# Two feed-forward blocks and a mixer on one core: a separate ring for the second products' left operands, exchanged accumulators, later transposes, and a last norm split in two

## The chip, the cores and the metric

The kernel runs on one core of a Trainium2 chip. The metric is device time in microseconds (us): 2611.52 us is the median of three runs of the kernel before (2611.07 to 2611.73). The profile is of one more execution, which took 2607.64 us, with 2605.9 us from its first instruction to its last.

## The reference

One trunk layer is computed for 128 context tokens and 1024 latent tokens of width 1024. Cut to what matters here:

```python
def _swiglu(h, w1, w2):                       # D_FF = 2816
    a, b = jnp.split(h @ w1, 2, axis=-1)
    return (jax.nn.silu(a) * b) @ w2

def _layer(x, mod, lw, rope, kv_ctx):
    sh1, sc1, g1, sh2, sc2, g2, sh3, sc3, g3 = [mod[:, i][:, None, :] for i in range(N_MOD)]
    f1 = _swiglu(_modulate(x, sh1, sc1), lw['ffn1_w1'], lw['ffn1_w2'])
    x = _layer_norm(ALPHA * x + 0.5 * g1 * f1, lw['ln_g'][0], lw['ln_b'][0])
    mix, k, v = _mixer(_modulate(x, sh2, sc2), lw, rope, kv_ctx)
    x = _layer_norm(ALPHA * x + g2 * mix, lw['ln_g'][1], lw['ln_b'][1])
    f2 = _swiglu(_modulate(x, sh3, sc3), lw['ffn2_w1'], lw['ffn2_w2'])
    x = _layer_norm(ALPHA * x + 0.5 * g3 * f2, lw['ln_g'][2], lw['ln_b'][2])
```

`_mixer` projects x, makes queries and keys with an RMS norm and a rotary turn, runs attention and a pooling branch, and projects the gated sum. Everything is float32.

## The kernel before

Every float32 operand is split into a high part (copied by ScalarE, L109) and a low part (subtracted by VectorE, L110), and each product is three matmuls (`mm3`, L132, L133, L134): high by high, high by low, low by high. `split` makes both parts, `transpose` (L137) is a matmul with the identity.

Each feed-forward block has an *up* stage and a *down* stage. The up stage makes silu(a)*b for the latent tokens with a Strassen scheme of seven products for a two by two blocking, and stores the parts and their sums (`keep_h`, `h_sums`: tiles `tmp`, `raw`, `pc`) to the tensor `h` in DRAM through POOL's DMA queue. The context tokens' feed-forward (`ctx_ffn`) runs in between as side work, advanced by `tick`. The down stage is h @ w2 with the same scheme: seven products M1, M5, M6, M7, M4, M3, M2 in this order, each of six groups; a group is two 128-row blocks of w2 for four row tiles, 24 matmuls of 128x512, and the last group one block, 12. For a group, `left` loads a part of h into a `raw` tile and splits it into two `so` tiles; `right` loads a piece of w2 into a `raw` tile, for M5 also a second one whose difference goes into a `tc` tile, and splits it into two `op` tiles. All these loads go through SP's queue in program order and share the five `raw` tiles of the pool `feed`. The last groups of a product (`tail`) are kept back and run tile by tile, and `done` takes the accumulators away. Each finished row tile is normed by `norm` in three steps, as side work, and the last product's norms in the last stage run at once.

The first down stage ends with `x_from_dram` as side work (`order`): it loads the normed x again into `raw` tiles, transposes it for the mixer and modulates it. The mixer's `queries` transposes the rotated queries `qr` just after they are made, and `ctx_attention` transposes the probabilities `pr` in the same way. The third norm stage ends the program.

What order the instructions have on an engine is decided when the program is built: the engines' queues are in order, pools hand out tiles in a ring, and a tile placed over the space of an older pool's tiles waits for the last use of those, a store's landing among them.

Of the kernel before, what the change touches and what calls it, by code (L numbers as in the profile page):

```python
# [25 lines left out]
F32 = mybir.dt.float32  # L26
F32R = mybir.dt.float32r
# [5 lines left out]
P = 128  # L33
D = 1024
# [20 lines left out]
class Layer:  # L55
# [203 lines left out]

    def modulate(self, slot, src, i, kc, g):  # L260
        m = self.raw_tile()[:, :GT]
        if g == 0:
            self.modulated(m[:, :P], src[:, :P], i, CTX, kc)
            self.modulated(m[:, P:], src[:, P:], i, LAT, kc)
        else:
            self.modulated(m, src, i, LAT, kc)
        self.split(slot[:, 0, :], slot[:, 1, :], m)

    def x_from_dram(self, src, i, g, out):
# [166 lines left out]
    def ctx_ffn(self, i, x, w1c, w1t, w2):  # L436
# [5 lines left out]
        for c in range(6):  # L442
# [5 lines left out]
            nc.scalar.activation(h[:, :n], banks[0][:, :n], AF.Silu)  # L448
            nc.vector.tensor_tensor(h[:, :n], h[:, :n], banks[1][:, :n], ALU.mult)
            if acc is None:  # L450
                acc = [self.bank(), self.bank()]
# [201 lines left out]
    def down(self, i, w2, h_d, norms, order, half, last):  # L653
# [3 lines left out]
        groups = [(f, min(2, 11 - f)) for f in range(0, 11, 2)]  # L657
        ops = lambda: self.pools["so"].tile([P, 1024], F32R, tag="so", name=self.name("so"), bufs=14 if last else 6)
        where = {"M1": 0, "M2": 2, "M4": 3, "M6": 4, "M5": 5, "M3": 6, "M7": 7}
        chain = [None] * len(groups)  # L660

        def left(name, g):
            c = groups[g][1]
            r = self.raw(h_d[g][:, where[name], :c, :], c * 512)
            hi, lo = ops()[:, : c * 512], ops()[:, : c * 512]
            self.split(hi, lo, r)
            return hi, lo
# [49 lines left out]
        yt = lambda: self.t([P, 2, 512], "y", bufs=8, pool=self.pools["y"])  # L717
        copy = lambda out, b: nc.scalar.activation(out, b, AF.Copy)
        X = [self.bank() for _ in range(4)]
        Y = [self.bank() for _ in range(4)]  # L720
        y1, y2 = ([yt() for _ in range(4)] for _ in range(2))
# [14 lines left out]

        def done1(j):
            add(y1[j][:, 0, :], Z[j], y1[j][:, 0, :])
            g = norm(half[0] + j, y1[j], fine=last and j == 3)
            if last:  # L740
                for _ in g:
                    pass
            else:
                self.add_side(g)

        if order:
            self.add_side(order())
        product("M2", Z, True, done1, tail=6 if last else 2, ticks=3)
        self.flush()
# [7 lines left out]
    def norms(self, i, res_of, dst):  # L757
# [7 lines left out]

        def norm(t, y, fine=False):
            y = self.flat(y)
            gate = gc if t == 0 else gl
            res = self.t([P, D], "res", bufs=2)
            with self.tc.issue_after(self.last_load):  # L770
                nc.sync.dma_start(res, res_of(t))
            rs = self.t([P, 1], "rs")
            mu = self.t([P, 1], "mu")
            nc.vector.tensor_tensor(y, y, gate, ALU.mult)
            yield
            nc.vector.scalar_tensor_tensor(y, res, ALPHA, y, ALU.mult, ALU.add, accum_out=mu)
            nc.vector.tensor_scalar(mu, mu, -1.0 / D, None, ALU.mult)  # L777
            nc.scalar.activation(res, y, AF.Square, bias=mu, accum_out=rs)
            nc.gpsimd.tensor_scalar(rs, rs, 1.0 / D, EPS, ALU.mult, ALU.add)
            nc.gpsimd.tensor_tensor(rs, rs, self.mhalf[:, 0:1], ALU.pow)  # L780
            yield
            for cs in [slice(0, 512), slice(512, D)] if fine else [slice(0, D)]:
                nc.vector.scalar_tensor_tensor(y[:, cs], y[:, cs], mu, lg[:, cs], ALU.add, ALU.mult)
                nc.vector.scalar_tensor_tensor(y[:, cs], y[:, cs], rs, lb[:, cs], ALU.mult, ALU.add)
                (nc.sync if last_stage(i) else nc.gpsimd).dma_start(dst(t)[:, cs], y[:, cs])
            yield

        return norm

    def ffn(self, i, head, res_of, dst, order, half, beside=None):  # L790
# [19 lines left out]
        with ExitStack() as st:  # L810
            self.open_pools(st, "down" + s, ("op", "tc", "so", "y", "rest") if i == 0 else ("op", "tc", "y", "rest", "so"))
            self.ph = self.pools["rest"]
            self.down(i // 2, a["w2_" + s], h_d, lambda: self.norms(i, res_of, dst), order, half, last_stage(i))
# [154 lines left out]
    def queries(self, g, acc, qg, pq):  # L968
        nc = self.nc
        for j in range(3):  # L970
# [13 lines left out]
            self.rope(qn, qr, self.rope_table(3 * g + j, 0, qg, pq), 8, pq)  # L984
            yield
            for h in range(2):
                b = self.bank()
# [134 lines left out]
    def ctx_attention(self, pool):  # L1122
        nc = self.nc
        for kvh in range(2):
# [15 lines left out]
            nc.vector.reciprocal(sm, sm)  # L1140
            nc.vector.tensor_tensor(pr, pr, sm.unsqueeze(2).broadcast_to([P, 4, P]), ALU.mult)
            yield
            b2 = self.bank()
# [148 lines left out]
    def run(self):  # L1292
# [3 lines left out]
        with ExitStack() as right:  # L1296

            def beside():
# [3 lines left out]
                0, self.head_input, lambda t: a["x"][self.rows(t)], lambda t: self.x1_d[t // 3][:, t % 3],  # L1302
                lambda: self.x_from_dram(self.x1_d, 1, 0, x), (5, 1), beside,
            )
# [39 lines left out]
def last_stage(i):  # L1344
    return i == 2
# [107 lines left out]
```

## Time and profile before

| | value |
|---|---|
| median of three runs | 2611.52 us (2611.07 to 2611.73) |
| the profiled execution | 2607.64 us |
| its span | 2605.9 us |
| mean granted TensorE clock | 0.976 |
| TensorE busy | 2481.7 us (95%) |
| VectorE busy | 1833.2 us (70%) |
| ScalarE busy | 1215.5 us (47%) |
| GpSimd busy | 458.4 us (18%) |

The span counts from the first to the last instruction; the profiled execution took 1.74 us more. TensorE idles for 124.2 us in all, and a granted clock of 0.976 means that for a part of the span its matmuls run at half speed. Every stage has its own pattern: the up stage of the first block ends at about 579 us, its down stage at 820, the mixer's input projection at 1265, its attention at 1560, its output at about 1855, the second up stage at 2358, and the second down stage's last matmul is at 2583. After that only the last norms run.

### The profile page before, as it was taken

How to read it: one execution, taken by the hardware profiler on the slowest of the kernel's cores; microseconds unless marked ns; L12 is line 12 of the kernel's file. 1: busy time of each engine (PE TensorE's matmuls, PEld its weight loads, DVE VectorE, ACT ScalarE, POOL GpSimd, SP SyncE). 2: the span in 40 equal slices, each digit the busy share in tenths (PEclk: the TensorE clock that was granted, in tenths of full speed). 3: DMA queues.
4: the chain of work that ended last, by engine and by line, in shares of the span. 5: the costliest groups of instructions: out<-in, count | busy, mean ns of one | idle time of the engine just before them, and what ended most of it. 6: DMA issues, size and time to landing. Idle time of an engine off the chain costs nothing.

```text
span 2605.9 us, 34155 instructions
## 1 busy us (share of the span) xinstructions
PE 2481.7 (95%) x12226; PEld 2133.9 (82%) x12226; DVE 1833.2 (70%) x2802; ACT 1215.5 (47%) x2086; POOL 458.4 (18%) x671
## 2 busy tenths in 40 slices
PE   7999999999998999999899999998999999999996
PEld 3788788877787989989899999997788788887775
DVE  4877688875686745577888876765777667666686
ACT  4644444434345343434578773433644444434442
POOL 0000001010011311132467640110000001110001
PEclk8999999999998999999999999999999999999998
DMA  7355567767666854445300024554455446558674
GB/s 283 113 181 179 165 229 237 245 229 235 208 225 236 234 174 165 162 150 174 109 1 2 1 78 164 202 209 156 139 196 180 159 165 238 198 195 266 231 234 141
DMA packets 164338, 461.64 MB, mean 177 GB/s; under 512 B 18804, under 2 KB 34932, under 8 KB 164168
## 3 DMA queue, kind: packets, MB, share of 16 engines
q1 hardware_dynamic: 143368, 383.63, 44.3%
q0 software_dynamic: 20800, 75.84, 8.0%
q8 instruction: 96, 1.57, 0.2%
q14 instruction: 74, 0.61, 0.1%
HBM read 388.32 MB, written 71.07 MB: 176 GB/s over the span
## 4 chain that ended last, share of the span: by engine, by line
PE 78%; DVE 8%; DMA 7%; issue 3%; ACT 2%; POOL 1%; SPq 1%; DVEq 0%; POOLq 0%; ACTq 0%
PE w L133 22%; PE w L132 22%; PE w L134 22%; PE w L861 7%; DMA raw<-w 4%; PE w L137 3%; DVE op L110 2%; DMA raw<-h 1%; DVE so L110 1%; DVE mx L1168 1%; DVE junk L192 1%; PE w L226 1%; DVE x L110 1%; DMA raw<-x 0%; SPq L113 0%
## 5 line engine op out<-in xcount | busy, mean ns | idle before, releaser
L109 ACT ACTIVATE op<-raw 128x1024 fp32r<-128x1024 f32 (+1 forms) x505 | 484.4, 970 | 606.2 <-PE w L133 265.2
L110 DVE TENSOR_TENSOR op<-raw,op 128x1024 fp32r<-128x1024 f32 (+1 forms) x505 | 558.6, 1113 | 267.3 <-ACT op L109 236.9
L132 PE MATMUL w<-b,op 128*128 128x512 f32 x880 | 342.4, 391 | 4.4 <-DVE tmp L546 2.4
L133 PE MATMUL w<-b,op 128*128 128x512 f32 x880 | 343.2, 390 | 0.3 <-DVE b L110 0.3
L134 PE MATMUL w<-b,op 128*128 128x512 f32 x880 | 341.4, 390 | 1.9 <-DVE op L110 1.9
L132 PE MATMUL w<-x,op 128*128 128x384 f32 x768 | 264.2, 345 | 4.3 <-ACT pin L1018 2.3
L134 PE MATMUL w<-x,op 128*128 128x384 f32 x768 | 261.0, 342 | 3.2 <-DVE mu L777 2.6
L133 PE MATMUL w<-x,op 128*128 128x384 f32 x768 | 261.9, 341 | 0.0
L134 PE MATMUL w<-op,so 128*128 128x512 f32 x616 | 244.2, 401 | 8.9 <-DVE so L110 8.9
L132 PE MATMUL w<-op,so 128*128 128x512 f32 x616 | 241.8, 401 | 8.8 <-ACT op L109 4.2
L133 PE MATMUL w<-op,so 128*128 128x512 f32 x616 | 245.5, 399 | 1.7 <-DVE op L110 1.7
L487 POOL DMA_DIRECT2D h<-tmp x80 | 43.5, 544 | 905.7 <-DVE tmp L551 440.5
L132 PEld LDWEIGHTS w<-b,op 128*128 128x128 f32 x880 | 165.7, 188 | 40.5 <-DVE tmp L546 3.3
L134 PEld LDWEIGHTS w<-b,op 128*128 128x128 f32 x880 | 165.5, 188 | 36.9 <-DVE op L110 2.3
L133 PEld LDWEIGHTS w<-b,op 128*128 128x128 f32 x880 | 165.6, 188 | 34.4 <-DVE b L110 0.6
L1181 POOL TENSOR_TENSOR pr<-pr,sm 128x384 f32<-128x384 f32 x192 | 157.5, 850 | 93.3 <-DVE sm L1179 75.8
L132 PE MATMUL w<-ax,op 128*128 128x512 f32 x352 | 136.1, 402 | 19.0 <-ACT ax L109 16.1
L132 PEld LDWEIGHTS w<-x,op 128*128 128x128 f32 x768 | 146.8, 191 | 6.2 <-ACT op L109 3.4
L192 DVE SCALAR_TENSOR_TENSOR junk<-raw,sil 128x1024 bf16<-128x1024 f32 x112 | 140.2, 1259 | 14.3 <-DMA raw<-w_mod 13.7
L134 PEld LDWEIGHTS w<-x,op 128*128 128x128 f32 x768 | 146.5, 191 | 3.9 <-DVE op L110 3.9
L134 PEld LDWEIGHTS w<-op,so 128*128 128x128 f32 x616 | 118.7, 193 | 37.5 <-DVE so L110 11.3
L132 PEld LDWEIGHTS w<-op,so 128*128 128x128 f32 x616 | 118.6, 193 | 36.8 <-ACT op L109 5.1
(269 smaller groups left out, 5098.2 us busy)
## 6 DMA issues: line engine op xcount, KB each, us to landing
raw<-w SPq DMA_DIRECT2D x240, 256.0 KB, 4.0
raw<-w SPq DMA_DIRECT2D x116, 512.0 KB, 4.2
raw<-h SPq DMA_DIRECT2D x92, 512.0 KB, 4.5
raw<-w1c SPq DMA_DIRECT2D x80, 512.0 KB, 4.5
raw<-w_mod SPq DMA_DIRECT2D x56, 512.0 KB, 4.3
raw<-w_gate SPq DMA_DIRECT2D x48, 512.0 KB, 4.2
h<-tmp POOLq DMA_DIRECT2D x80, 256.0 KB, 4.0
h<-pc POOLq DMA_DIRECT2D x52, 256.0 KB, 4.5
```

The lines of the kernel that those rows point to most:

```text
L109: self.nc.scalar.activation(hi, src, AF.Copy)
L110: self.nc.vector.tensor_tensor(lo, src, hi.bitcast(F32), ALU.subtract)
L132: mm(out, lhsT=lh, rhs=rh, start=start, stop=False)
L133: mm(out, lhsT=lh, rhs=rl, start=False, stop=False)
L134: mm(out, lhsT=ll, rhs=rh, start=False, stop=stop)
L137: self.nc.tensor.transpose(out, src, self.ident)
L192: nc.vector.scalar_tensor_tensor(junk, w, 1.0, self.sil[cond], ALU.mult, ALU.mult, accum_out=self.mod[:, cond, b : b + 1],)
L226: nc.tensor.matmul(acc[:2, :256], lhsT=self.sil_t[:, :, lo + k], rhs=w[:, k, :], start=lo + k == 0, stop=lo + k == KC - 1,)
L487: self.nc.gpsimd.dma_start(h_d[f // 2][:, 2 * kh + n, f % 2, :], h)
L861: self.nc.tensor.matmul(acc[h][j], lhsT=lhs[:, part, js], rhs=w[wi][:, h * 512 : (h + 1) * 512], start=f, stop=l)
L1168: nc.vector.tensor_reduce(mx[:, c : c + 1], b[:, :GT], AX.X, ALU.max)
L1181: nc.gpsimd.tensor_tensor(pr[:, c, :], pr[:, c, :], sm[:, 3:4].broadcast_to([P, GT]), ALU.mult)
```

## The change

The left operands of the down stages' products are loaded into a ring `sr` of their own (three tiles in the first stage, four in the last) in place of `raw` tiles. The `op` ring of the down stages has 6 tiles in the first and 12 in the last (8 before in both), and the `so` ring of the last stage 12 (14 before), so the pools lie in other places. The accumulators X and Y are allocated in the other order. The first stage's side work at its end becomes `x_early`, which loads x through POOL's queue into a ring `xr` of two, waits for eight ticks, and transposes in eight steps during M2. `queries`, `ctx_attention` and `ctx_ffn` get one more `yield` each, by which their transposes come one tick later. In the last stage tile 3's norm is split: `last` multiplies what is already summed by the gate and adds the residual, for each half of the row, before M2, and `finish` multiplies M2's accumulator by the gate, adds it and does what is left of the norm, in halves; its y goes out by the queues of SP and ScalarE. The other norms store through POOL's queue.

```diff
+    def x_early(self, src, i, out, wait):
+        t = lambda tag, n: self.pools["xr"].tile([P, n], F32, tag=tag, name=self.name(tag), bufs=2)
+        def load(q):
+            r = t("xr", 768)
+            self.nc.gpsimd.dma_start(r.rearrange("p (a b) -> p a b", a=3), src[0][:, :, q * 256 : (q + 1) * 256])
+            return r
+        r = [load(0), load(1)]
+        for _ in range(wait):
+            yield
+        for q in range(4):
+            for k in range(2):
+                b = self.bank()
+                for j in range(3):
+                    self.transpose(b[:, j * P : (j + 1) * P], r[q][:, j * 256 + k * P : j * 256 + (k + 1) * P])
+                s = self.xslot()
+                self.modulate(s, b[:, :GT], i, 2 * q + k, 0, t("xm", GT))
+                out.append(s)
+                if k and q < 2:
+                    r.append(load(q + 2))
+                yield
...
@@ ctx_ffn
             nc.vector.tensor_tensor(h[:, :n], h[:, :n], banks[1][:, :n], ALU.mult)
+            yield
...
@@ down
-        ops = lambda: self.pools["so"].tile([P, 1024], F32R, tag="so", name=self.name("so"), bufs=14 if last else 6)
+        ops = lambda: self.pools["so"].tile([P, 1024], F32R, tag="so", name=self.name("so"), bufs=12 if last else 6)
...
-            r = self.raw(h_d[g][:, where[name], :c, :], c * 512)
+            r = self.pools["sr"].tile([P, 1024], F32, tag="sr", name=self.name("sr"), bufs=4 if last else 3)[:, : c * 512]
+            self.load(r.rearrange("p (a b) -> p a b", a=c), h_d[g][:, where[name], :c, :])
...
+        Y = [self.bank() for _ in range(4)]
         X = [self.bank() for _ in range(4)]
-        Y = [self.bank() for _ in range(4)]
...
         def done1(j):
+            if last and j == 3:
+                finish(Z[j])
+                return
             add(y1[j][:, 0, :], Z[j], y1[j][:, 0, :])
-            g = norm(half[0] + j, y1[j], fine=last and j == 3)
+            g = norm(half[0] + j, y1[j])
...
+        def last(t, y):
+            tt, stt = nc.vector.tensor_tensor, nc.vector.scalar_tensor_tensor
+            res = residual(t)
...
+            for (v, cs), out in zip(halves, (None, m2)):
+                tt(v, v, gl[:, cs], ALU.mult)
+                stt(v, res[:, cs], ALPHA, v, ALU.mult, ALU.add, accum_out=out)
+            def finish(b):
+                z = res[:, c0]
+                tt(z, b, gl[:, c0], ALU.mult)
+                stt(y0, z, 1.0, y0, ALU.mult, ALU.add, accum_out=mu)
+                nc.vector.tensor_scalar(mu, mu, m2, -1.0 / D, ALU.add, ALU.mult)
+                nc.scalar.activation(res, self.flat(y), AF.Square, bias=mu, accum_out=rs)
+                for v, cs in halves:
+                    stt(v, v, mu, lg[:, cs], ALU.add, ALU.mult)
+                nc.gpsimd.tensor_scalar(rs, rs, 1.0 / D, EPS, ALU.mult, ALU.add)
+                nc.gpsimd.tensor_tensor(rs, rs, self.mhalf[:, 0:1], ALU.pow)
+                for (v, cs), q in zip(halves, (nc.sync, nc.scalar)):
+                    stt(v, v, rs, lb[:, cs], ALU.mult, ALU.add)
+                    q.dma_start(dst(t)[:, cs], v)
+            return finish
...
@@ ffn
-            self.open_pools(st, "down" + s, ("op", "tc", "so", "y", "rest") if i == 0 else ("op", "tc", "y", "rest", "so"))
+            self.open_pools(st, "down" + s, ("op", "tc", "so", "y", "sr", "xr", "rest") if i == 0 else ("op", "tc", "sr", "y", "rest", "so"))
+            self.op_bufs = 6 if i == 0 else 12
...
@@ queries
             yield
+            if j == 0:
+                yield
...
@@ ctx_attention
             nc.vector.tensor_tensor(pr, pr, sm.unsqueeze(2).broadcast_to([P, 4, P]), ALU.mult)
+            yield
             yield
...
@@ run
-                lambda: self.x_from_dram(self.x1_d, 1, 0, x), (5, 1), beside,
+                lambda: self.x_early(self.x1_d, 1, x, 8), (5, 1), beside,
```

Three places show how instructions move. The first is VectorE's queue where the first down stage begins. `pc_851` and `pc_852` are the last sums of h that the up stage makes, `op_880` and `op_886` are low parts of right operands, `so_889` that of a left operand (group 3 of M1), and `tc_909` is the first difference of M5's. Before:

```order
568 L110 TENSOR_TENSOR op_880_4674<-raw_878_4670,op_879_4673 128x1024
569 L110 TENSOR_TENSOR op_886_4711<-raw_884_4707,op_885_4710 128x1024
570 L502 TENSOR_TENSOR pc_851_4580<-tmp_848_4529,raw_850_4575 128x512
571 L502 TENSOR_TENSOR pc_852_4583<-tmp_845_4509,raw_850_4575 128x512
572 L110 TENSOR_TENSOR op_892_4748<-raw_890_4744,op_891_4747 128x1024
573 L110 TENSOR_TENSOR so_889_4741<-raw_887_4738,so_888_4740 128x1024
```

And now, where `so_871`, `so_877` and `so_883` are the left operands' low parts of M1's groups 0, 1 and 2 (before, they stood ahead of row 568):

```order
566 L110 TENSOR_TENSOR op_886_4717<-raw_884_4713,op_885_4716 128x1024
567 L527 TENSOR_TENSOR pc_851_4580<-tmp_848_4529,raw_850_4575 128x512
568 L527 TENSOR_TENSOR pc_852_4583<-tmp_845_4509,raw_850_4575 128x512
569 L707 TENSOR_TENSOR tc_909_4855<-raw_910_4856,raw_908_4852 128x1024
570 L110 TENSOR_TENSOR so_871_4636<-sr_869_4633,so_870_4635 128x1024
571 L110 TENSOR_TENSOR so_877_4673<-sr_875_4670,so_876_4672 128x1024
572 L110 TENSOR_TENSOR so_883_4710<-sr_881_4707,so_882_4709 128x1024
573 L707 TENSOR_TENSOR tc_917_4897<-raw_918_4898,raw_916_4894 128x1024
574 L110 TENSOR_TENSOR so_889_4747<-sr_887_4744,so_888_4746 128x1024
575 L110 TENSOR_TENSOR op_892_4754<-raw_890_4750,op_891_4753 128x1024
```

The low parts of M1's left operands moved behind the stage's last sums of h and behind a difference for M5 (rows 569 and 573), which needs two loads of w2. The load of `raw_910` waits on SP for `pc_852` and for the landing of the store of `raw_850`, whose place it takes.

The second place is ScalarE's queue where the last down stage begins; `tmp_4018` is the up stage's last silu, the `so` tiles are left, the `op` tiles right operands' high parts. Before:

```order
1744 L550 ACTIVATE tmp_4018_21139<-w_4002_20984 128x512
1745 L109 ACTIVATE so_4039_21194<-raw_4038_21192 128x1024
1746 L109 ACTIVATE op_4042_21201<-raw_4041_21198 128x1024
1747 L109 ACTIVATE so_4045_21231<-raw_4044_21229 128x1024
1748 L109 ACTIVATE op_4048_21238<-raw_4047_21235 128x1024
```

And now:

```order
1744 L575 ACTIVATE tmp_4018_21147<-w_3997_20974 128x512
1745 L109 ACTIVATE so_4039_21205<-sr_4038_21203 128x1024
1746 L109 ACTIVATE so_4045_21242<-sr_4044_21240 128x1024
1747 L109 ACTIVATE so_4051_21279<-sr_4050_21277 128x1024
1748 L109 ACTIVATE so_4057_21316<-sr_4056_21314 128x1024
1749 L109 ACTIVATE so_4063_21353<-sr_4062_21351 128x1024
1750 L109 ACTIVATE so_4069_21366<-sr_4068_21364 128x512
1751 L109 ACTIVATE op_4042_21212<-raw_4041_21209 128x1024
```

The first right operand moved behind all six left ones. On VectorE its low part `op_4043` follows in the same way, and its place was that of the tile `pc_4021`, so it waits for the landing of that tile's store.

The third place is TensorE's queue in the first down stage, where M2 begins; `w_1117` to `w_1120` are its four accumulators. Before:

```order
3110 L134 MATMUL w_1120_6030<-op_1125_6040,so_1123_6034 128x512
3111 L137 MATMUL w_1128_6070<-ident_75,raw_1127_6068 128x128 x3
3112 L137 MATMUL w_1131_6080<-ident_75,raw_1127_6068 128x128 x3
3113 L137 MATMUL w_1135_6092<-ident_75,raw_1134_6090 128x128 x3
3114 L137 MATMUL w_1144_6139<-ident_75,raw_1134_6090 128x128 x3
3115 L137 MATMUL w_1148_6151<-ident_75,raw_1147_6149 128x128 x3
3116 L137 MATMUL w_1151_6161<-ident_75,raw_1147_6149 128x128 x3
3117 L132 MATMUL w_1117_6027<-op_1142_6111,so_1139_6104 128x512
```

And now:

```order
3111 L137 MATMUL w_1141_6152<-ident_75,xr_1127_6074 128x128
3112 L132 MATMUL w_1117_6033<-op_1133_6087,so_1130_6080 128x512
3113 L132 MATMUL w_1118_6034<-op_1133_6087,so_1130_6080 128x512
3114 L132 MATMUL w_1119_6035<-op_1133_6087,so_1130_6080 128x512
3115 L132 MATMUL w_1120_6036<-op_1133_6087,so_1130_6080 128x512
3116 L137 MATMUL w_1141_6152<-ident_75,xr_1127_6074 128x128 x2
3117 L137 MATMUL w_1150_6199<-ident_75,xr_1127_6074 128x128 x3
3118 L137 MATMUL w_1154_6211<-ident_75,xr_1128_6076 128x128
3119 L133 MATMUL w_1117_6033<-op_1134_6088,so_1130_6080 128x512
```

Of the eighteen transposes that stood ahead of M2's first group seven are still there, the others moved behind later groups of it (eleven in rows 3187 to 3190, six more in rows 3221 and 3222 with the six that followed later before).

## Rows read from the trace of the kernel before

**Rows 1.** The profile page, its first line.

```profile
span 2605.9 us, 34155 instructions
```

**Rows 2.** Stages: window, length, busy by engine, clock, DMA share, GB/s.

```profile
579.00:820.00 241.00, 223.20 (x948) 181.74 (x948) 152.91 (x161) 101.23 (x132) 18.00 (x20) 0.96 0.67 226
2584.00:2605.90 21.90, 0.00 (x0) 0.00 (x0) 17.04 (x24) 4.97 (x8) 6.64 (x8) 0.60 0.42 144
```

**Rows 3.** What TensorE waited for: line, releaser, total us, times, longest us.

```profile
PE w L137 <- DMA raw<-x: 13.9, 5, 7.2
PE w L134 <- DVE so L110: 8.9, 4, 3.4
PE w L137 <- DVE qr L932: 6.5, 3, 3.1
PE w L137 <- DVE pr L1141: 4.6, 1, 4.6
PE w L132 <- DVE y L725: 2.9, 2, 2.3
PE w L134 <- DVE mu L777: 2.6, 1, 2.6
```

**Rows 4.** TensorE's timeline, first down stage: start, us, instruction, idle before.

```profile
579.49 1.20 PE L132 MATMUL w<-op,so 128*128 128x512 f32 x4 [1.63 <-ACT op L109]
582.47 0.63 PE L133 MATMUL w<-op,so 128*128 128x512 f32 x1
582.89 0.63 PE L134 MATMUL w<-op,so 128*128 128x512 f32 x1
```

**Rows 5.** Short stretches, columns as in rows 2.

```profile
579.40:593.60 14.20, 13.66 (x52) 10.87 (x53) 9.34 (x10) 5.81 (x7) 2.37 (x4) 0.88 0.82 280
584.60:593.60 9.00, 9.00 (x41) 7.47 (x40) 4.14 (x4) 3.88 (x4) 1.11 (x2) 0.99 0.96 332
784.00:799.00 15.00, 7.77 (x31) 6.35 (x29) 7.17 (x10) 11.13 (x22) 0.00 (x0) 0.77 0.66 199
1118.00:1128.20 10.20, 7.11 (x29) 6.73 (x28) 7.66 (x11) 3.73 (x8) 4.62 (x7) 0.67 0.34 109
```

**Rows 6.** DMA issues, 581.5 to 590: transfer, queue, count, KB, median landing us.

```profile
raw<-w SPq DMA_DIRECT2D x4, 256.0 KB, 4.0
h<-raw POOLq DMA_DIRECT2D x1, 512.0 KB, 4.4
h<-pc POOLq DMA_DIRECT2D x2, 256.0 KB, 6.3
```

**Rows 7.** Timeline of POOL's queue and VectorE, first down stage.

```profile
581.98 0.72 POOL L499 DMA_DIRECT2D h<-raw  x1 [1.91 <-DVE raw L498]
588.91 1.22 DVE L110 TENSOR_TENSOR so<-raw,so 128x1024 fp32r<-128x1024 f32 x1
607.02 1.23 DVE L681 TENSOR_TENSOR tc<-raw,raw 128x1024 f32<-128x1024 f32 x1 [3.96 <-DMA raw<-w]
614.71 1.22 DVE L681 TENSOR_TENSOR tc<-raw,raw 128x1024 f32<-128x1024 f32 x1 [4.10 <-DMA raw<-w]
```

**Rows 8.** Timeline of three engines, start of the last down stage.

```profile
2360.65 0.80 PE L133 MATMUL w<-op,so 128*128 128x512 f32 x1 [1.24 <-DVE op L110]
2361.65 1.29 DVE L502 TENSOR_TENSOR pc<-tmp,raw 128x512 f32<-128x512 f32 x2
2362.63 0.57 POOL L503 DMA_DIRECT2D h<-pc  x1 [2.15 <-DVE pc L502]
```

**Rows 9.** Timeline of four engines, end of the program.

```profile
2582.92 0.40 PE L134 MATMUL w<-op,so 128*128 128x512 f32 x1
2598.11 1.15 ACT L778 ACTIVATE res<-y,mu 128x1024 f32<-128x1024 f32 x1 [3.49 <-DVE mu L777]
2600.27 0.94 POOL L780 TENSOR_TENSOR rs<-rs,mhalf 128x1 f32<-128x1 f32 x1
2601.24 1.42 DVE L784 SCALAR_TENSOR_TENSOR y<-y,rs,nc 128x512 f32<-128x512 f32 x2 [0.44 <-POOL rs L780]
```

More of the change, by code (lines that the diff above doesn't have):

```diff
@@ L258, in mod_part, with modulate @@
         yield
-    def modulate(self, slot, src, i, kc, g):
-        m = self.raw_tile()[:, :GT]
+    def modulate(self, slot, src, i, kc, g, m=None):
+        m = self.raw_tile()[:, :GT] if m is None else m
         if g == 0:
@@ L747, in down @@
             self.add_side(order())
+        if last:
+            finish = norm.last(half[0] + 3, y1[3])
         product("M2", Z, True, done1, tail=6 if last else 2, ticks=3)
@@ L764, in norms, with residual, norm @@
                 nc.sync.dma_start(t, self.gate_d[i][cond].rearrange("k p -> (k p)").partition_broadcast(P))
-        def norm(t, y, fine=False):
+        def residual(t):
+            if last_stage(i):
+                res = self.t([P, D], "tc", bufs=6, pool=self.pools["tc"])
+            else:
+                res = self.t([P, D], "res", bufs=2)
+            with self.tc.issue_after(self.last_load):
+                nc.sync.dma_start(res, res_of(t))
+            return res
+        def last(t, y):
+            tt, stt = nc.vector.tensor_tensor, nc.vector.scalar_tensor_tensor
+            res = residual(t)
+            rs, mu, m2 = (self.t([P, 1], n) for n in ("rs", "mu", "mu2"))
+            halves = [(y[:, h, :], slice(h * 512, (h + 1) * 512)) for h in range(2)]
+            (y0, c0), (y1, c1) = halves
+            for (v, cs), out in zip(halves, (None, m2)):
[15 more added lines that the diff above has]
+            return finish
+        def norm(t, y):
             y = self.flat(y)
             gate = gc if t == 0 else gl
-            res = self.t([P, D], "res", bufs=2)
-            with self.tc.issue_after(self.last_load):
-                nc.sync.dma_start(res, res_of(t))
+            res = residual(t)
             rs = self.t([P, 1], "rs")
@@ L781, in norm @@
             yield
[L782 to L785, printed above, removed]
+            nc.vector.scalar_tensor_tensor(y, y, mu, lg, ALU.add, ALU.mult)
+            nc.vector.scalar_tensor_tensor(y, y, rs, lb, ALU.mult, ALU.add)
+            nc.gpsimd.dma_start(dst(t), y)
             yield
+        norm.last = last
         return norm
```

## The prediction

> **What bounds the kernel now.** I read the page first, then the busy time by stage, then what TensorE waits for, and last the timelines at the places that the change moves. The span is 2605.9 us [rows 1], and the profiled execution 2607.64 us. TensorE is busy for 95% of it, so the time is TensorE's matmuls plus its idle time (124.2 us) plus what its clock costs after idle time. A change that adds and removes no matmul, as this one, can only move the last two, and the end: behind the last matmul, at 2582.92 + 0.40 = 2583.32 us, 22.6 us of norms follow [rows 2, 9]. In the first down stage TensorE is busy for 223.2 of 241 us [rows 2].
>
> The clock matters because of what follows each longer wait. In [rows 4] two neighbours start 0.42 us apart, after idle time; later 41 matmuls take 9.00 us, 0.22 us each [rows 5]. These are the two levels, 1.2 and 2.4 GHz. The mean clock of 0.88 over 14.2 us [rows 5] is 0.12 x 14.2 / 0.5 = 3.4 us at the lower one. In such a stretch 8 matmuls are started where 15.5 could be: 1.6 us lost. The mean of 0.96 over the first down stage's 241 us [rows 2] is 19 us, six such stretches: one at its start, two around the x transposes (0.77 over 15 us is 6.9 us, [rows 5]), and three that I give to its other longer waits.
>
> **The change part by part.**
>
> *Start of the first down stage: -11.5 us.* The order on VectorE has `tc_909` ahead of `so_871` now, and TensorE can start 8 matmuls of M1 before it needs `so_871`. `tc_909` needs `raw_910`, whose load waits for the store of `raw_850`: issued at 581.98 [rows 7], landed 4.4 us later [rows 6], at 586.4. The two halves of the load are issued then and land 4.0 us after [rows 6], the second somewhat later: about 591. The difference and `so_871` take 1.22 us each [rows 7]: 593.5. By 593.6 before had started 52 matmuls [rows 5]; 44 fewer at 0.22 us are 9.7 us. Idle time of that length brings at least one more slow stretch than the one there: 1.6. Sum 11.3, which I take as 11.5, from 9.7 up to 14 if two stretches are added.
>
> *The rest of it: +13.7.* TensorE's four waits for `so` make 8.9 us [rows 3], all in this stage, behind SP's queue, where the loads of h stand among those of w2 for five tiles. With `sr` they no longer do, and three slow stretches go with them: 8.9 + 3 x 1.6 = 13.7. What is late next is the ladder below. Bounds: 3 (only the ring's share goes) to 14.5.
>
> *x transposed later: +9.4.* The wait for `raw<-x` of 7.2 us [rows 3] has its place between M3 and M2. Now only 7 of 18 transposes stand there, on the first two loads, and the rest behind three groups and more. Two slow stretches go, a part of which was idle, so 2.2 instead of 3.2. Cover: the later loads have about 30 matmuls, 6.6 us, against 4.4 us for 512 KB [rows 6]. Loads in POOL's queue have the norms' small operations and stores in front of them; if that delays the first two, up to 5 us come back. Range 4 to 10.4.
>
> *Start of the mixer's projection: +2.* Its wait for VectorE's norms is 2.6 us [rows 3] with a stretch behind it, 4.2 at most. x is modulated earlier now, but VectorE's norms remain; I take half.
>
> *Queries: +10.* The waits for `qr` sum to 6.5 us [rows 3], of which two are 3.1 us. About 24 matmuls of 128x384 are between now: at three quarters of 0.22 us, 0.165 us, they are 4.0 us, more than 3.1. The stretch around the second has a clock of 0.67 over 10.2 us [rows 5]: 6.7 us, two stretches; I take one for the first. 6.2 + 3 x 1.6 = 11; some of it lies in idle time, so 10 (6.2 to 11).
>
> *Context attention: +5.6.* One wait of 4.6 us [rows 3], covered with 24 matmuls for 4.0, and a stretch of 1.6.
>
> *The yield in `ctx_ffn` and other orders of the up stages: 0*, within 3 either way: its own wait is under 1 us, and where side work falls differently a wait may come or go.
>
> *Start of the last down stage: -10.* ScalarE copies all six left operands before the first right one, and the low part `op_4043` waits for the store of `pc_4021` to land. Before, the first matmul that needs it starts at 2360.65, and the stores are issued from 2362.63, the second 0.6 us later [rows 8]. With 6.3 us, as in the first stage [rows 6], it lands at 2369.5; 1.2 for the subtraction gives 2370.7: 10.0 later. With 4.4 us it would be 8, with one more slow stretch 11.6.
>
> Here the Trainium skill would have it shorter: "DMA: Bandwidth & Descriptors", section "Anatomy of one DMA", gives a fit of about 2 us plus the bytes at 436 GB/s for a transfer issued from GpSimd, by which 256 KB land in an estimated 2.6 us. Then this term would be about -6.3 us and the forecast 3.7 us lower. The rows have 6.3 us while loads run, and I go by them.
>
> *The rest of the last stage: +2.* Twelve `op` tiles hold six groups, and the wait behind a `done` (2.3 us, [rows 3]) with its stretch may go: 0 to 3.9. M2 tile by tile needs all six groups early, a risk of 3.
>
> *The end: +11.* M2 now finishes a tile after 33 matmuls, 7.3 us apart, where the four tiles ended almost together. A whole norm has on VectorE about 0.7 + 4 x 1.22 us, under 7.3, so tiles 0 to 2 are hidden, but for one operation of tile 2 that stands in tile 3's way. Behind the last matmul: a half multiply, that operation and a half add, 0.7 + 1.22 + 0.7, some 0.6 for hops and the mean, and then what is there before from the square on, 2605.9 - 2598.11 = 7.8 us [rows 1, 9]. In all 11.0 instead of 22.6, so 11.6; I take 11 (8 to 12).
>
> *X and Y exchanged, stores by POOL's queue:* 0. TensorE waits for operands, not for a bank, and the last y doesn't go by POOL; if tile 3's two POOL operations stand behind a store's issue there, 1 us.
>
> **Sum.** -11.5 + 13.7 + 9.4 + 2 + 10 + 5.6 - 10 + 2 + 11 = +32.2 us. 2607.64 - 32.2 = 2575.4 for an execution like the profiled one. The median of the runs shown is 3.9 us above it, so I forecast 2579 us.
>
> **The rivals.**
>
> *The ladder.* In the new order each group of M1 from the fourth on has a difference of M5 in front, and each difference waits for a load that waits for the difference before it. Such a ladder is seen before in M5: the differences start at 607.02 and 614.71, 7.7 us apart, each after some 4 us of waiting for `raw<-w` [rows 7]. A group's 24 matmuls take 24 x 0.22 = 5.3 us. So it costs 2.4 us a group, less a lead of two groups. Over M1 and M5 it is up to 13 us, and the forecast becomes 2592. For it speaks that a group then needs 2.1 MB, 6.3 us at the 332 GB/s of the fullest stretch [rows 5]; against it, that the right operands of M1 are loaded before.
>
> The Trainium skill says the same in "DMA: Bandwidth & Descriptors", section "Issuing engines are not separate DMA queues": all transfers end on the same 16 engines and interleave, whoever issues them, so a further ring or queue brings no bandwidth. The share of 0.96 in that stretch [rows 5], with loads and stores from two queues in it, agrees.
>
> *Slower.* The same ladder through the whole first down stage, since M6 and M7 hang on the differences too. With 2.4 us a group it eats the 32 us from the 14th group on; through 24 groups it costs 58 and ends at 2637. Against it: M6 needs one load for a difference, and before M6 and M7 show fewer waits than this.
>
> *Cheap starts.* With fewer loads at the same time the stores land sooner, the two starts cost 10 us in place of 21.5, and the time is 2567.
>
> *The transposes gain little.* A later transpose only meets a later operand, since side work comes in the same sequence: half of the 27 us for x, queries and context attention stay away: 2592. Against it stands the order, which has 24 to 30 matmuls in between.
>
> **How the numbers follow.** Forecast 0.52, ladder in M1 and M5 0.2, cheap starts 0.13, transposes 0.08, slower 0.07. The forecast's own range is 2570 to 2588. With cheap starts on one side and the ladder on the other, 2562 to 2600 holds 8 in 10. A measurement of this kernel tells 0.2%, 5.2 us, from no change. Below 2606.3 lie all cases but the slower one and a tail in which ladder and transposes meet: faster 0.89, no change 0.05, slower 0.06.
>
> **What would show it.** TensorE's first wait for `so` in the first down stage should be about 9 to 11 us long and end near 593 on before's scale, the start of the last down stage should show a wait for `op` of about 10 us, no wait for `raw<-x` should stand at the first stage's end, and those for `qr` and `pr` should be gone. The end should follow the last matmul by about 11 us. The forecast is wrong if waits for `so` recur in M1 and M5 every 5 to 8 us, or if M2 of the last stage waits for operands.

## The result and the profile after

The changed kernel takes 2588.09 us, the median of four runs (2585.16 to 2590.84), beside 2611.62 us for the kernel before. The ratio is 0.9908 (0.9891 to 0.9926): faster by 0.9%, by 23.5 us where 32.5 were forecast. That is 0.1 us above the forecast's own range of 2570 to 2588 and inside the wider one of 2562 to 2600. In five later runs of the same kernel on one chip the times were 2577.78 to 2586.91, so single times differ by more than the 0.2% that the prediction took as the limit, and 5 us between two kernels below are read from traces before they are read from times. Two kernels below have one execution each at a far lower clock (4138.53 and 3531.07 us), which is left out of their times, and the profile of the first of them is of that execution and is not read.

The profiled execution took 2585.16 us. What answers to rows 1 and 2 is the page's first line and the busy time behind the last matmul, by stretch (length, then busy time of PE, PEld, DVE, ACT and POOL, clock, DMA share, GB/s):

```profile
span 2583.4 us, 34069 instructions
```

```profile
2573.00:2583.40 10.40, 0.00 (x0) 0.00 (x0) 5.39 (x9) 1.24 (x2) 2.84 (x4) 0.65 0.25 101
```

From the last matmul's end it is 11.0 us long now, 22.6 before [rows 2, 9]. What TensorE waited for (releaser, total us, times, longest us):

```profile
...
PE w L132 <- ACT op L109: 18.8, 7, 11.6
PE w L133 <- DVE op L110: 14.5, 4, 7.3
PE w L137 <- DMA raw<-x: 9.8, 6, 4.0
PE w L134 <- DVE so L110: 9.6, 1, 9.6
PE w L134 <- DVE op L110: 5.8, 3, 3.1
PE w L132 <- ACT so L109: 4.5, 1, 4.5
PE w L132 <- DVE tmp L571: 4.4, 3, 2.8
...
PE w L137 <- DVE dl L110: 2.8, 1, 2.8
PE w L137 <- DVE mx L1241: 2.3, 1, 2.3
...
PE w L137 <- DVE qr L998: 0.5, 2, 0.3
```

Beside [rows 3] the reader sees what went (6.5 us for `qr` are 0.5, the wait of 7.2 us for `raw<-x` is gone, that for `pr` too, four waits for `so` are one) and what came: one wait of 9.6 us for `so`, one of 11.6 us for `op`, and longer ones for `op` in L133.

The same matmul can be found in both traces, since every stage has the same number of them. The table gives the start of some in both (us from the span's start); its last column is the difference between one row's gain and the row before's, so it tells what a stretch won or lost.

| matmul | before | after | gain so far | in this stretch |
|---|---|---|---|---|
| last of the first up stage | 577.47 | 582.25 | -4.8 | -4.8 |
| 25th of M1 | 587.38 | 607.12 | -19.7 | -15.0 |
| last of M3, first down stage | 777.30 | 782.04 | -4.7 | +15.0 |
| first of the mixer | 820.39 | 816.56 | +3.8 | +8.6 |
| 101st of the mixer | 844.15 | 839.13 | +5.0 | +1.2 |
| last of the attention (`w<-kv,qh`) | 1539.75 | 1523.53 | +16.2 | +11.2 |
| first transpose of the second block | 1805.17 | 1788.55 | +16.6 | +0.4 |
| first `w<-b,op` of its up stage | 1852.36 | 1839.49 | +12.9 | -3.8 |
| last of its up stage | 2355.25 | 2344.40 | +10.9 | -2.0 |
| 25th of the last M1 | 2368.03 | 2366.23 | +1.8 | -9.1 |
| last of all | 2582.92 | 2572.00 | +10.9 | +9.1 |
| end of the span | 2605.9 | 2583.4 | +22.5 | +11.6 |

The start of the first down stage, on TensorE and then on VectorE (start, us, instruction, idle before and its end):

```profile
587.16 0.79 PE L132 MATMUL w<-op,so 128*128 128x512 f32 x1 [4.53 <-ACT so L109]
600.59 0.79 PE L134 MATMUL w<-op,so 128*128 128x512 f32 x1 [9.65 <-DVE so L110]
```

```profile
588.71 1.28 DVE L527 TENSOR_TENSOR pc<-tmp,raw 128x512 f32<-128x512 f32 x2
598.17 1.23 DVE L707 TENSOR_TENSOR tc<-raw,raw 128x1024 f32<-128x1024 f32 x1 [8.18 <-DMA raw<-w]
599.32 1.22 DVE L110 TENSOR_TENSOR so<-sr,so 128x1024 fp32r<-128x1024 f32 x1
```

VectorE stands before the difference `tc` for 8.18 us until a load of w2 has landed, and the low part `so` behind it releases TensorE. The first wait, of 4.53 us, is for ScalarE, which makes three copies of right operands ahead of the first left one:

```profile
583.23 2.94 ACT L109 ACTIVATE op<-raw 128x1024 fp32r<-128x1024 f32 x3
586.07 2.94 ACT L109 ACTIVATE so<-sr 128x1024 fp32r<-128x1024 f32 x3
```

In the stretch of these waits the clock is lower than in any of [rows 5]:

```profile
586.00:606.60 20.60, 9.79 (x22) 7.23 (x23) 8.62 (x9) 3.00 (x4) 1.82 (x3) 0.50 0.70 238
```

At 0.50 all 20.6 us are at 1.2 GHz, the waits in them included, with only 22 matmuls.

The start of the last down stage, on TensorE, ScalarE and VectorE:

```profile
2356.42 2.08 PE L132 MATMUL w<-op,so 128*128 128x512 f32 x4 [11.63 <-ACT op L109]
2359.08 0.79 PE L133 MATMUL w<-op,so 128*128 128x512 f32 x1 [0.59 <-DVE op L110]
```

```profile
2354.79 0.63 ACT L109 ACTIVATE so<-sr 128x512 fp32r<-128x512 f32 x1 [2.08 <-DMA sr<-h]
2355.32 1.04 ACT L109 ACTIVATE op<-raw 128x1024 fp32r<-128x1024 f32 x1
```

```profile
2357.80 4.63 DVE L110 TENSOR_TENSOR op<-raw,op 128x1024 fp32r<-128x1024 f32 x4 [1.66 <-DMA h<-pc]
```

ScalarE copies the sixth left operand, for whose load it waits, and only then the first right one, and this is what TensorE's 11.63 us wait for. VectorE's low part of it waits until the store of `pc` has landed, which adds 0.59 us on TensorE. That store took 5.3 us from its issue (the DMA issues from 2348 to 2356):

```profile
h<-pc POOLq DMA_DIRECT2D x2, 256.0 KB, 5.3
```

So it is nearer to the 6.3 us of [rows 6] than to the 2.6 us that are estimated by the Trainium skill's fit ("DMA: Bandwidth & Descriptors", "Anatomy of one DMA"); with other transfers in flight (DMA share 0.94 from 2348.8 to 2357.7) the fit is half of the time. Where few were in flight it comes close: a store of the same size, issued at 2346.45 with a DMA share of 0.29, landed after 2.3 us.

The end, on TensorE and VectorE:

```profile
2572.00 0.40 PE L134 MATMUL w<-op,so 128*128 128x512 f32 x1
```

```profile
2572.77 0.68 DVE L819 TENSOR_TENSOR tc<-w,nc 128x512 f32<-128x512 f32 x1
2573.58 1.28 DVE L848 SCALAR_TENSOR_TENSOR y<-y,rs,nc 128x1024 f32<-128x1024 f32 x1
2574.78 0.68 DVE L820 SCALAR_TENSOR_TENSOR y<-tc,y 128x512 f32<-128x512 f32 x1
```

This is the sum of the prediction in order: a half multiply, tile 2's operation, a half add. From the last matmul's end at 2572.40 to the span's end it is 11.0 us.

### The profile page after: what moved, and what is told of

Read it like the earlier page. It is cut to its first block, busy times and chain, and to the rows that moved or that the text cites. A ratio compares the mean times of both kernels' runs of the same rounds, so it can differ in the third digit from the quotient of the medians.

```text
span 2583.4 us, 34069 instructions
## 1 busy us (share of the span) xinstructions
PE 2464.7 (95%) x12226; PEld 2125.0 (82%) x12226; DVE 1830.9 (71%) x2806; ACT 1211.7 (47%) x2086; POOL 459.1 (18%) x683
## 5 line engine op out<-in xcount | busy, mean ns | idle before, releaser
L133 PE MATMUL w<-b,op 128*128 128x512 f32 x880 | 342.9, 390 | 0.3 <-DVE b L110 0.3
L133 PE MATMUL w<-x,op 128*128 128x384 f32 x768 | 260.2, 339 | 0.0
L132 PE MATMUL w<-op,so 128*128 128x512 f32 x616 | 239.4, 398 | 17.0 <-ACT op L109 11.6
L133 PE MATMUL w<-op,so 128*128 128x512 f32 x616 | 242.5, 394 | 0.6 <-DVE op L110 0.6
L133 PEld LDWEIGHTS w<-b,op 128*128 128x128 f32 x880 | 165.5, 188 | 34.2 <-DVE b L110 0.6
L109 ACT ACTIVATE so<-sr 128x1024 fp32r<-128x1024 f32 x84 | 82.4, 986 | 192.1 <-PE w L133 125.3
L132 PEld LDWEIGHTS w<-op,so 128*128 128x128 f32 x616 | 117.6, 191 | 42.1 <-ACT op L109 12.1
```

The source lines that it names most:

```text
L109: self.nc.scalar.activation(hi, src, AF.Copy)
L132: mm(out, lhsT=lh, rhs=rh, start=start, stop=False)
L133: mm(out, lhsT=lh, rhs=rl, start=False, stop=False)
```

## The experiments

The theory after the result was: the starts of the down stages cost as much as the new ring gives in the products behind them, the places of the pools and the order that follows from them are the reason, the yields in the mixer are worth about 12 us, and the yield in `ctx_ffn` costs. Rivals are with each run. Ratios are to the kernel before.

**The ring taken back.** `left` loads into `raw` again, both down stages have 8 `op` tiles, the last one 14 `so` tiles.

```diff
-            r = self.pools["sr"].tile([P, 1024], F32, tag="sr", ...)[:, : c * 512]
-            self.load(r.rearrange("p (a b) -> p a b", a=c), h_d[g][:, where[name], :c, :])
+            r = self.raw(h_d[g][:, where[name], :c, :], c * 512)
...
-            self.op_bufs = 6 if i == 0 else 12
+            self.op_bufs = 8
...
```

> The changed kernel with the left operands' loads back in the raw tiles, 8 op tiles in both down stages, 14 so tiles in the last and the pools in the order of before; all other parts of the change stay. Theory: in the two traces the starts of the down stages cost 15 and 9 us and the products after them give 15 and 9 us back, so the ring with its pools is worth nothing: 2588 us, within 4, with waits of 2 to 3 us at both starts and the waits for so in M5 to M7 as before. Rival 1: the ring is a net gain, since the starts are late for another reason (the up stage's end): 2597 to 2610. Rival 2: the ring is a net loss as in the prediction's sum (2.2 - 8): about 2582.

Measured: 2604.15 us, 0.9962 (0.9949 to 0.9975). The theory's total of 2588 was wrong, and the first rival's number came out, but not by its mechanism. Both starts do return to short waits:

```profile
594.45 1.20 PE L132 MATMUL w<-op,so 128*128 128x512 f32 x4 [1.69 <-ACT op L109]
...
2353.44 1.20 PE L132 MATMUL w<-op,so 128*128 128x512 f32 x4 [2.58 <-ACT op L109]
```

Counted by matmuls as above, against the changed kernel, they give back 16.5 and 10.2 us, and the products behind them lose 17.3 and 13.4 us, with five waits for `so` again:

```profile
PE w L134 <- DVE so L110: 12.3, 5, 3.2
```

What the theory had left out lies elsewhere: behind the last matmul (at 2581.76) are 20.2 us instead of 11.0, and the first up stage ends 10.1 us later, with 8.3 us of waits for `tmp` where the changed kernel has 4.4. How much of the latter is the ring's is not shown: single traces differ there, and in the run without the mixer's yields, whose edit lies behind that stage, it ends 5.9 us later too. The 12 `op` tiles are part of what the ring's change gives, at the end above all.

**Other places for the pools.**

```diff
-            self.open_pools(st, "down" + s, ("op", "tc", "so", "y", "sr", "xr", "rest") if i == 0 else ("op", "tc", "sr", "y", "rest", "so"))
+            self.open_pools(st, "down" + s, ("op", "tc", "y", "so", "sr", "xr", "rest") if i == 0 else ("op", "tc", "y", "sr", "rest", "so"))
-            self.op_bufs = 6 if i == 0 else 12
+            self.op_bufs = 6 if i == 0 else 8
```

> The changed kernel with other places for the pools: first down stage op, tc, y, so, sr, xr, rest (y before so), last stage op, tc, y, sr, rest, so with 8 op tiles instead of 12; nothing else. By its order the low parts of the left operands stand ahead of the first difference of M5, and left and right operands alternate in the last stage. Theory: the starts' cost comes from tiles that lie over late tiles of the up stage and from the order that follows, so it goes without the gain of the ring: 15 and 9 us less, 2564 to 2570, waits under 3 us at both starts. Rival: the starts wait for transfers anyway (the loads of w2 and h themselves), so at most 5 us: 2583 or more. The slow stretches of the clock after the first start (20 us at half) should shrink to 7 us or less by the theory.

Measured: 2586.07 us, 0.9903 (0.9884 to 0.9923). By its total the rival was right; by its trace the starts are mended. TensorE waits 0.24 us for the first low left part instead of 9.65, and the clock of the same 20.6 us is 0.83 instead of 0.50:

```profile
592.25 0.80 PE L134 MATMUL w<-op,so 128*128 128x512 f32 x1 [0.24 <-DVE so L110]
```

```profile
586.00:606.60 20.60, 18.13 (x68) 14.35 (x69) 12.14 (x12) 8.08 (x9) 1.82 (x3) 0.83 0.85 287
```

The starts gave 11.5 and 10.2 us, M1 to M4 took 5 back, and the last matmul is 15.4 us earlier than in the changed kernel. The end took it back: with 8 `op` tiles M2's tiles end 1.8 us apart again (4.6 to 8.1 in the changed kernel), and VectorE is busy with four norms for the whole of it (16.0 of 20.5 us):

```profile
2557.00:2577.50 20.50, 0.00 (x0) 0.00 (x0) 15.98 (x23) 4.96 (x8) 8.19 (x11) 0.57 0.25 103
```

**No yields in the mixer.** The added `yield` is taken out of `queries` and of `ctx_attention`.

```diff
-            if j == 0:
-                yield
...
-            yield
             yield
             b2 = self.bank()
```

> The changed kernel without the added yield in queries and in ctx_attention. Theory: the waits for qr (3.1 us twice, with their slow stretches) and for pr come back as before; between the mixer's first matmul and the attention the change gained 12 us, so 2598 to 2602. Rival: the transposes' waits only moved (the changed kernel has new waits of 2 to 3 us for op, dl and mx at the end of the projection), so that the yields are worth under 5 us: 2593 or less.

Measured: 2601.3 us, 0.995 (0.9932 to 0.9968), as the theory expected. The old waits are back:

```profile
PE w L137 <- DVE qr L998: 7.5, 4, 3.2
...
PE w L137 <- DVE pr L1207: 4.7, 1, 4.7
```

The last matmul is 10.1 us later than in the changed kernel. Only 6.6 us of this arise between the mixer's first matmul and the attention's last, so the theory's 12 us are not borne out by the trace: the first up stage, ahead of the edit, ended 5.9 us later, of which 4.2 were left at the mixer. From the mixer's first matmul to the attention's last it takes 713.6 us here, 719.4 before, and 706.1 to 712.2 in the nine traces read with the yields, so the 6.6 us are uncertain by several, and that the total agrees is in part luck.

**No yield in `ctx_ffn`.**

```diff
             nc.vector.tensor_tensor(h[:, :n], h[:, :n], banks[1][:, :n], ALU.mult)
-            yield
             if acc is None:
```

> The changed kernel without the added yield in ctx_ffn. Theory: that yield shifts side work in both up stages and is the cause of the 5 us that the first up stage lost and of a part of the 6 us lost in the second one's lead and body: 2580 to 2583. Rival: the loss comes from the slow gate stores (the wait for them is 5.9 and 7.3 us instead of 3.4 and 5.1) and differs from run to run: 2588 within 3, and the spread of single times stays.

Measured: 2575.35 us (2574.43 to 2578.42), 0.9858 (0.9838 to 0.9878). That is 12.7 us below the changed kernel's first four times, with an interval apart from theirs, and 6.1 us below its five later ones, whose interval (0.986 to 0.9908) overlaps. The theory was right, and more than it said: one line costs some 10 us (10.7 at the last matmul of the two traces). The waits of L133 behind the slow stores of the gates (10.6 us and more to land in the kernel before) are 3.4 us in both up stages (3.40 and 5.08 before the change):

```profile
277.80 0.80 PE L133 MATMUL w<-op,pc 128*128 128x512 f32 x1 [3.40 <-DVE op L110]
...
2038.26 0.72 PE L133 MATMUL w<-op,pc 128*128 128x512 f32 x1 [3.38 <-DVE op L110]
```

In the changed kernel they are these:

```profile
279.19 0.80 PE L133 MATMUL w<-op,pc 128*128 128x512 f32 x1 [5.89 <-DVE op L110]
...
2045.56 0.80 PE L133 MATMUL w<-op,pc 128*128 128x512 f32 x1 [7.30 <-DVE op L110]
```

The rival had the right place, but not chance: the traces of six kernels and runs with the yield show 4.8 to 6.4 us at the first of the two, those without it 3.3 to 3.4. The first up stage lasts 505.2 to 516.1 us in these six traces and 499.5 to 504.4 in the five without the yield. One step of it can be read on VectorE. In both kernels the sum `ts` follows a load that lands at 276 us; with the yield a product `tmp` and a second sum stand ahead of the low part for which TensorE waits:

```profile
276.10 0.69 DVE L544 TENSOR_TENSOR ts<-raw,raw 128x512 f32<-128x512 f32 x1 [8.72 <-DMA raw<-w]
276.71 0.68 DVE L576 TENSOR_TENSOR tmp<-tmp,tmp 128x512 f32<-128x512 f32 x1
277.31 0.68 DVE L545 TENSOR_TENSOR ts<-raw,ts 128x512 f32<-128x512 f32 x1
277.91 2.35 DVE L110 TENSOR_TENSOR op<-raw,op 128x1024 fp32r<-128x1024 f32 x2
```

Without it, the low part comes 1.4 us earlier:

```profile
275.92 0.69 DVE L543 TENSOR_TENSOR ts<-raw,raw 128x512 f32<-128x512 f32 x1 [8.09 <-DMA raw<-w]
276.53 1.22 DVE L110 TENSOR_TENSOR op<-raw,op 128x1024 fp32r<-128x1024 f32 x1
```

The wait for `tmp` of 2.8 us at the first up stage's end goes with it too.

**The last start, with the 12 tiles kept.** Without the yield in `ctx_ffn`, the last stage's pools are `("tc", "y", "rest", "sr", "op", "so")`.

> The changed kernel without ctx_ffn's added yield, and in the last down stage the pools in the order tc, y, rest, sr, op, so with the 12 op tiles kept; the first stage as in the changed kernel. Left and right operands alternate at the last stage's start again. Theory: in the run with other pools the first matmul that needs a low right part came 10 us earlier, and with 8 op tiles M2 no longer ran tile by tile, so that the tail went from 11 back to 21 us; with 12 tiles in a better place the 9 to 10 us are kept and the tail stays at 11: 2575.4 - 9 = 2566. Rival: the end needs the places too, or the loads of w2 and h at the start take the time that ScalarE gave free: 2572 or more.

Measured: 2561.6 us, 0.9803 (0.9776 to 0.9829): 13.8 us below the kernel that is only without the yield, more than the theory's 9.4.

**Both starts.** The same, with `("op", "tc", "y", "so", "sr", "xr", "rest")` in the first stage.

> As the kernel with the last stage's pools moved, and in the first down stage y ahead of so too. Theory: the first start gets the 11.5 us that it got in the earlier run, of which M1 to M5 took back 4.6 by waits for right operands, so 7 us below the kernel with the last start alone: about 2559. Rival: the ladder of differences, once M1 starts earlier, takes all of it back: the same within 2 us.

Measured: 2558.5 us (2554.91 to 2563.67), 0.9795 (0.9769 to 0.9821), the best of all: 2.05% below the kernel before, and 23 us below the changed one that ran beside it. Against the run with the last start alone it is 3.1 us, between theory and rival and within what single times differ by. The trace has the ladder that takes a part back, two waits in M1 and M5 that the changed kernel, which starts later, doesn't have:

```profile
610.84 0.50 PE L133 MATMUL w<-op,so 128*128 128x512 f32 x1 [1.43 <-DVE op L110]
621.03 0.50 PE L133 MATMUL w<-op,so 128*128 128x512 f32 x1 [3.10 <-DVE op L110]
```

The first start is not mended whole: TensorE's first wait there, for ScalarE's first left copy, is still 4.47 us, and the 25th matmul of M1 comes 12.6 us behind the last of the up stage, 9.9 before the change. The first matmuls of the last down stage wait as before again, 1.1 us for the low right part where [rows 8] have 1.24:

```profile
2327.22 1.35 PE L132 MATMUL w<-op,so 128*128 128x512 f32 x4 [2.58 <-ACT op L109]
2329.66 0.80 PE L133 MATMUL w<-op,so 128*128 128x512 f32 x1 [1.08 <-DVE op L110]
```

**x by the old way.** The changed kernel with `x_from_dram` in place of `x_early`.

```diff
-                lambda: self.x_early(self.x1_d, 1, x, 8), (5, 1), beside,
+                lambda: self.x_from_dram(self.x1_d, 1, 0, x), (5, 1), beside,
```

> The changed kernel with the side work of before at the end of the first down stage (x loaded into raw tiles by SP's queue, transposed at once); all else as changed. Theory: the wait of 7.2 us ahead of M2 comes back with its slow stretches, 8.6 us: 2596 to 2598. Rival: with the left operands in sr, raw tiles are free earlier, so the loads of x come in time without x_early: 2590 or less.

Measured: 2586.06 us, 0.9905 (0.9883 to 0.9926), beside 2581.44 for the changed kernel on the same chip. By times the theory's 8.6 us can't be told from the rival's 2 or less. By the trace it can: between the last matmuls of M3 and the first of the mixer the changed kernel is 7.8 us quicker, and the waits stand where they stood, now 6.0 us in two parts:

```profile
790.74 0.85 PE L137 MATMUL w<-ident,raw 128*128 128x128 f32 x6 [2.42 <-DMA raw<-x]
795.15 1.51 PE L137 MATMUL w<-ident,raw 128*128 128x128 f32 x6 [3.57 <-DMA raw<-x]
```

**The changed kernel again.**

> The changed kernel itself, beside the others on the same chip: 2588 within 3 us. Its four times shown so far lie in two pairs, 2585 to 2586 and 2590 to 2591; if the pairs are of the gate stores' landing, this profile shows a wait for op of 3.4 or of 5.9 us near 280 us.

Measured: 2581.44 us (2577.78 to 2586.91), 0.9884 (0.986 to 0.9908). That is 6.6 us below the 2588 expected and outside the 3 us given. The two pairs of times were no pattern: five more times lie between and below them. In its profile the wait near 280 us is 5.36 us.

**The last norm whole.** From the kernel with both starts mended, `last` and `finish` are taken out; M2 still runs tile by tile.

```diff
-            if last and j == 3:
-                finish(Z[j])
-                return
             add(y1[j][:, 0, :], Z[j], y1[j][:, 0, :])
-            g = norm(half[0] + j, y1[j])
+            g = norm(half[0] + j, y1[j], fine=last and j == 3)
...
```

> The kernel with both starts mended, but tile 3's norm is made whole behind M2's end as in the kernel before (gate, residual, mean, square, then halves), while M2 still runs tile by tile with 12 op tiles. Theory: most of the end's gain is from M2 by tiles, since the two runs with 8 op tiles had 20 us behind the last matmul with the split norm; the split takes a whole multiply and a whole add (2 x 1.22 us) down to two halves and one half add: 12.2 + 1.9 = 14 us behind the last matmul, 2560. Rival: the split is what counts: 20 us or more, 2566.

Measured: 2562.3 us, 0.981 (0.9782 to 0.9839). Behind the last matmul are 12.8 us, against 12.2 with the split in the same kernel. The theory was right in kind, and by the traces the split is worth 0.6 us, less than the 1.9 expected; the times, 3.8 us apart, can't tell.

**X and Y as before.** From the same kernel, X is allocated ahead of Y.

> The kernel with both starts mended and the accumulators X and Y allocated in the order of before. Theory: TensorE waits for operands and not for banks, so nothing moves: 2558.5 within 3 us and no wait at a product's start that isn't there with the exchange. Rival: M1 or M5 waits for a bank that the up stage's last copy still reads: 2 to 5 us more.

Measured: 2558.28 us, 0.9808 (0.9792 to 0.9825) beside 2558.5. The exchange does nothing that shows.

## Why the prediction was right, and where its sum was off

The sign and most mechanisms held, and the time came out at the upper edge of the range; of the 32.2 us in the sum 22.5 came. That it is no further off is in part luck, since a loss of 10.6 us put at 0 was met by 7.1 us more than counted in the last stage. Point by point:

- *Start of the first down stage*, -11.5 (bounds 9.7 to 14): measured -15.0, outside. The chain was as worked out, store, load, difference, low part. Two sizes were off. The store took 6.0 us to land where 4.4 were counted and the loads behind it 5.2 where about 4.6 were, so that the low part was ready at 595.8 on before's scale instead of 593.5. And the 16 matmuls behind the wait lost about 3 us to the lower clock, where 1.6 were counted. The wait of 4.53 us for ScalarE's first copy was not foreseen; it lies within the time of this chain, but stays when the chain is mended.
- *The rest of that stage*, +13.7: +15.0. The run without the ring lost 17.3 in its products.
- *x transposed later*, +9.4: +8.6, and 7.8 in the run that undid it.
- *Mixer's start, queries, context attention*, +17.6: +12.4. The waits went as said, but "cover" was counted only for the transposes. New waits came at the end of the projection, 2.66 and 3.15 us for `op`, and behind it, 2.8 for `dl` and 2.3 for `mx`. The run without the yields puts them at 6.6 us by its trace.
- *The yield in `ctx_ffn`*, 0 within 3: the step that was most wrong. The first up stage lost 4.8 us and the second block's lead and up stage 5.8; the run without it is 10.7 us earlier at the last matmul, 3.1 and 5.9 of them from these stretches. The prediction looked at the wait that the yield covers (0.8 us), and not at what moves behind it: side work shares the queues with the products, and the matmuls behind the slow gate stores then wait longer.
- *Start of the last down stage*, -10: -9.1. Both steps that were named are there, but the sum went by the store's landing, and the trace by ScalarE's order: 11.63 us for its copy, then 0.59 for the low part behind the store. That the two ended so close together is chance.
- *The rest of it*, +2 (0 to 3.9): +9.1. The prediction counted one wait behind a `done` and gave it to the 12 `op` tiles. In the trace both such waits are gone (1.66 and 2.28 us before, for `y`) with what the clock lost behind them, and this goes with the ring, not with the 12 tiles: from its 25th matmul to its last the stage takes 205.8 us with the ring and 12 `op` tiles, 205.8 with the ring and 8, 219.2 with 8 and no ring, and 214.9 before.
- *The end*, +11: +11.6. Right in size, but the credit belongs to M2 by tiles: two kernels with the split norm and 8 `op` tiles have 20.2 and 20.5 us there, and one with the whole norm and 12 tiles has 12.8.
- *X and Y*, 0: 0.

Of the rivals the ladder is real, but not where it was put. In the changed kernel M1 runs without a wait from its 25th matmul on (19.7 us behind throughout), since the late start gives the loads their lead. It shows where M1 starts early: 1.4 and 3.1 us. The Trainium skill's rule that another queue brings no bandwidth ("DMA: Bandwidth & Descriptors", "Issuing engines are not separate DMA queues") fits that: with the same loads, an earlier M1 only waits later. The slower rival, the cheap starts and the transposes that gain little didn't happen.

What stays open: how the other order that the extra yield brings adds up to some 10 us (VectorE's queue shows 1.4 us of it), and why single times of one kernel differ, by 13 us over nine runs of the changed one and by 4 to 9 us for those without the yield.

## What to carry to other kernels

A pool that is moved or grown can put the first tile of the next stage over the last tile of the stage before; then a store's landing, and the order that is built around it, stand at the head of an in-order queue. Look at the first instructions of a stage on each engine, and lay what is needed last over what is freed last: here the pools' order in one line is worth 17 us (2575.35 against 2558.5).

A part that is thought to be free should be run without: one `yield` took some 10 us (10.7 by the traces, 6 to 13 by the times) from the 33 that the other parts gained.

## What the runs showed of the hardware that was not expected

Around the 9.65 us wait TensorE was at 1.2 GHz for 20.6 us on end: from ahead of the stage's first matmul, through the wait, and for 6 us behind it. In the kernel before, waits of 1.63 and 0.45 us at this place went with 3.4 us of it. With the long wait gone (0.24 us), the clock's mean over the same 20.6 us was 0.83. The 22 matmuls in it were busy for 9.79 us where 0.22 us each is 4.8, so the long waits cost their own length and about 5 us more.

A store of 256 KB took 5.3 to 6.3 us to land while loads were running and 2.3 us when few were, and the tile that it read was not free before.
